# Keys, queries and cached values moved in more and smaller transfers

## The chip, the cores and the metric

The kernel runs on one core of a Trainium2 chip. The core has five engines that take their instructions in order, each from its own queue, and wait for one another on semaphores: TensorE (PE) multiplies matrices, VectorE (DVE), ScalarE (ACT) and GpSimd (POOL) do elementwise work, and SyncE (SP) only issues transfers between memory (DRAM) and the core's SBUF. The transfers themselves run on 16 DMA engines that all queues share. The metric is the device time of one launch in microseconds (us), the median of several runs; less is better.

## The reference

The reference is one inference step of a decoder trunk with two layers, for a prompt of 1024 tokens and eight samples of one token each that share the weights. Layer 0 is a convolution module beside a spatial gating unit; layer 1 is sparse attention with 16 query heads on 4 key and value (kv) heads of 64 numbers. Each layer is followed by an MLP. All is float32.

The part that matters here is layer 1. One projection gives queries, and keys and values for three branches, and three gates per head:

```python
z = h @ w_in
q, ck, cv, sk, sv, wk, wv, g = jnp.split(z, splits, axis=-1)
q_rot = rope(q, pos)
return q, q_rot, kvr(ck), kvr(cv), rope(kvr(sk), pos), kvr(sv), rope(kvr(wk), pos), kvr(wv), gates
```

Attention is a gated sum of three softmaxes: of the plain queries over compressed keys, of the rotated queries over the eight best blocks of 64 keys, and of the rotated queries over a window of 512 keys:

```python
o = g[..., 0:1] * o_cmp + g[..., 1:2] * o_sel + g[..., 2:3] * o_win
```

The samples do the same over paged caches and a window buffer of 512 rows, and the step returns that buffer moved on by one row (`kw[:, -nw:]`, `vw[:, -nw:]`).

## The kernel before

Features lie on the 128 partitions and tokens along the rows, so an activation is eight tiles of 128x1032 (1024 prompt tokens and 8 samples). A float32 product is made of three matmuls on numbers split in a high and a low part (`dense`, L278): for each weight tile 8 tiles of K x 3 chunks of tokens x 3 passes. Weights come through `granule` (L178): SP loads a raw tile (L180), ACT makes its high part (L175), POOL its low part (L176); nine slots, so three granules, are in the ring at once. All other SBUF tiles are slots of equal size, handed out the longest free first (`Slots`), so that the load of a tile waits for whoever last used its slot.

The order of the work on each engine is set when the kernel is built: a scheduler runs the program against a model of the chip and places each engine's instructions in one fixed order. SP issues its transfers in that order, and each of them waits, beside its data and its slot, on one of eight counters (DMAHW0 to DMAHW7) that SP's transfers use in turn.

Layer 1 goes in these steps:

- `project`: the tiles of the compressed branch, which are stored in DRAM (`cd`, L812); the keys of the selected and the window branch, two tiles each (the two halves of a head, four kv heads of 32 rows in a tile), rotated, split and written to DRAM as `kd` (L851); the queries, four groups of two tiles, of which the plain ones go to `qp` (L874) and the rotated ones, high and low part, to `qd` (L876). These writes are the spills. A tile holds (kv, r) on its partitions; in DRAM the kv head is outermost, so that later one kv head can be read by itself.
- Still in `project`: values and gates, nine tiles of tokens in three groups, each for two weights (`pvg`, L895 to L897), and in between `prompt_compress`, twice, which reads `cd` back as `pch` (L763) and its weights as `w1r` (L616) and multiplies them (`pc`, L641).
- `prompt_attention`: 32 units, of one kv head and 128 queries each, eight for a kv head. `load_k` (L950) loads the four key tiles of a kv head: window and selected, high and low part. Each has the 64 rows of the head twice, one copy below the other, since the queries carry their high parts over their low parts. The next head's keys are loaded at the end of the eighth unit. `load_q` loads a unit's queries (`pc<-qp` L962, `q<-qd` L964). The scores are `S<-K,q` (L1045), the values are multiplied one unit later (`tp` L1088, `op` L1102).
- `sample_attention`: its steps are spread over the units. `fetch_wv` loads the window's values (`wvr`, L1249), and POOL stores them moved on by one row to output 17 (L1252, L1253, L1255).

Of the kernel before, what the change touches and what calls it, by code (L numbers as in the profile page):

```python
# [15 lines left out]
P = 128  # L16
# [3 lines left out]
B = 8  # L20
# [11 lines left out]
class Slots:  # L32
    """Equal pieces of SBUF, handed out in the order of the trace, the longest free first."""
# [21 lines left out]
def body(tc, I, O, ctx):  # L55
# [48 lines left out]
    # One of a layer's six vectors at a time, over eight tiles of K: four groups of rows at once, for the halves  # L104
    # of its columns and for even and odd tiles.
# [30 lines left out]
    def ada_half(a):  # L136
        """Half of a vector's tiles."""
        l, j, h, ws, pl = a
        if h == 0:
            half_p[0] = mmps("pada")  # L140
        for n in (0, 2):
            ada_mm(half_p[0], 4 * h + n, ws[n:n + 2])
        pl.put(ws)
        if h == 1:
            ada_end(l, j, half_p[0])

    def ada_steps(vectors, pl):
        """Vectors (layer, number) two tiles at a time."""
        todo = [(l, j, k) for l, j in vectors for k in range(0, KT, 2)]

        def fetch(l, j, k):
            return [ada_raw(l, j, k + i, pl) for i in range(2)]

        ws = fetch(*todo[0])
        for n, (l, j, k) in enumerate(todo):
            if k == 0:
                p = auxps("pada")
            ada_mm(p, k, ws)
            pl.put(ws)
            if n < len(todo) - 1:  # L160
                ws = fetch(*todo[n + 1])
            else:
                ring.free.extend(pl.free)
            if k == KT - 2:
                ada_end(l, j, p)
            yield
# [19 lines left out]
    class Norm:  # L186
        """RMS norm of x, a chunk at a time; h = x * rstd * scale + shift as hi and lo parts, or the output."""
# [82 lines left out]
    def dense(pt, wh, wl, xh, xl, ks, woff, chunks, only=None):  # L270
        """pt[c] = W^T x over the tiles ks of K, the float32 product in three passes."""
        for n, k in enumerate(ks):
            if only not in (None, k):
                continue
            w0 = woff + k * 128
            for i, (w, v) in enumerate(((wh, xh), (wh, xl), (wl, xh))):
                for c in chunks:
                    pe.matmul(pt[c][:, :CH], w[:, w0:w0 + 128], v[k][:, c * CH:(c + 1) * CH],  # L278
                              start=n == 0 and i == 0, stop=n == len(ks) - 1 and i == 2)

    def lead(srcs, names):
        """Two tiles right after a norm: its last chunk comes last."""
        w = [granule(s) for s in srcs]
        pts = [[mmps(n) for _ in range(3)] for n in names]
        for pt, (wh, wl) in zip(pts, w):
            dense(pt, wh, wl, hh, hl, range(KT), 0, (0, 1))
        for k in range(KT):
            for pt, (wh, wl) in zip(pts, w):
                dense(pt, wh, wl, hh, hl, range(KT), 0, (2,), k)
        ring.put(*[t for p in w for t in p])  # L290
        return pts

    def resid(l, gi, mt, pt, c, first):
        """x += gate * y for one tile of features and one chunk."""
# [92 lines left out]
    def even(half):  # L387
# [62 lines left out]
        for i in range(4):  # L450
            # the samples: one position each
# [13 lines left out]
        for g in range(4):  # L465
            # keep s <= t (s on partitions)
            pool.affine_select(wsT[:, g, :], wsT[:, g, :], pattern=[[1, P]], compare_op=OP.is_ge, fill=0.0, base=0,
                               channel_multiplier=-1)
# [3 lines left out]
        # u  # L472
# [15 lines left out]
        def conv_norm(c):  # L488
            """Layer norm over the 512 channels of the convolution, silu."""
# [27 lines left out]
        # v, with the tokens on partitions  # L517
# [5 lines left out]
        def v_norm(tl):  # L523
            """Layer norm over the channels of a group's token tiles."""
# [78 lines left out]
    cmp_bias = {}  # L603

    def cmp_weights(kv, eng=None):
        """The compression's first weights as hi and lo parts, and the bias that its position term adds."""
# [26 lines left out]
    def compress_half(q, w, ch, jh):  # L633
        """The compression's hidden units [e, (k, c)], the part of half of the positions' pairs; ch: its (hi, lo)."""
# [16 lines left out]
    kcd = tc.dram_tile([P, 1024], FT, name="kcd")     # samples' compressed keys: (kv, r); b, half, c  # L651
    vcd = tc.dram_tile([P, 1024], FT, name="vcd")     # and values: (b % 2, c); b // 2, kv, d
# [3 lines left out]
    def gather(dst, src, i, q=None):  # L656
        """One page of a pool; src: the pool, its pages first."""
# [8 lines left out]
    class Units:  # L666
        """The compression of the samples' pages, one of keys and values and one sample at a time, in halves."""
# [16 lines left out]
        def prep(self, eng=None):  # L684
            """The next half of the positions' pairs as hi and lo parts."""
# [22 lines left out]
        def run(self):  # L708
            """Half a unit."""
# [34 lines left out]
    qd = tc.dram_tile([4, 2, 2, 32, 4, S], FR, name="qd").bitcast(FT)        # rotated: kv, hl, half, r, g, token  # L744
    qp = tc.dram_tile([4, 2, 2, 32, 2, S], FT, name="qp")                    # plain: kv, g // 2, half, r, g % 2, token
    kd = tc.dram_tile([2, 2, 4, 2, 32, S], FR, name="kd").bitcast(FT)        # sel/win, hl, kv, half, r, token
    cd = tc.dram_tile([2, 2, 2, 256, 512], FR, name="cd").bitcast(FT)        # k/v, hl, j2, (kv d), (jp c)
# [36 lines left out]
    def project(R):  # L784
# [3 lines left out]
        R["ks"] = cst.tile([P, 2, 2, B], FT, name="ks")         # half, sel/win, b  # L788
        R["cks"] = cst.tile([P, 4, B], FT, name="cks")
        R["qs"] = cst.tile([P, 2, 2, 4, B], FT, name="qs")      # rot/plain, half, g, b  # L790
# [8 lines left out]
        # the compressed branch's rows  # L799
# [18 lines left out]
        def rope(pa, pb, c, a1, a2, r1, r2, t):  # L818
            """The rotated halves of one chunk; a1, a2: copies of the plain ones."""
# [10 lines left out]
        for w in range(2):  # L830
# [18 lines left out]
            for half in range(2):  # L849
                for m in range(2):  # L850
                    sp.dma_start(kd[w, m, :, half], h[half][m][:, :S].bitcast(FT))  # L851
# [3 lines left out]
        # queries  # L855
        for g in range(4):
# [16 lines left out]
            for i in range(2):  # L873
                sp.dma_start(qp[:, g // 2, i, :, g % 2], qa[i][:, :S])  # L874
                for m in range(2):
                    sp.dma_start(qd[:, m, i, :, g], h[i][m][:, :S].bitcast(FT))  # L876
# [3 lines left out]
        # values and gates, with the tokens on partitions  # L880
# [34 lines left out]
    def topk_bias(out, score, nb, m8, mr):  # L915
        """out: 0 for the eight largest scores (ties: the lower index first), else -1e30."""
# [6 lines left out]
    def prompt_attention(R, psb):  # L923
# [21 lines left out]
        def load_k(kv):  # L945
            K = {}
            for w in (1, 0):
                for m in range(2):
                    t = sl.get("K", FR)
                    sp.dma_start(t[:, :S].bitcast(FT),  # L950
                                 kd[w, m, kv].rearrange("a r t -> (a r) t")[None].to_broadcast([2, 64, S]))
# [3 lines left out]
        def load_q(n):  # L955
            """The queries of the nth unit: rotated, hi over lo; plain, two heads over two."""
# [11 lines left out]
        class Unit:  # L968
            """The four heads of one kv head and 128 queries, the queries on partitions."""
# [57 lines left out]
            def score(self, w, g):  # L1027
                """One head's probabilities, in the window (w = 1) or the selected blocks."""
# [45 lines left out]
            def values(self):  # L1074
                """The steps of the product with the values."""
# [47 lines left out]
        def turned(i):  # L1123
            """The heads of the first kv heads again, as hi and lo parts."""
# [47 lines left out]
    def sample_attention(R, bank):  # L1172
        """All heads of the samples' one position: rows (b, h) on partitions. The steps, in their order: arithmetic
        and, in between, the fetches of what comes two steps later."""
# [68 lines left out]
        def fetch_wv(pp):  # L1243
            vr = held["wv", pp] = [sl.get("wvr") for _ in range(4)]
            for bp in range(4):
                v4 = vr[bp][:, :1024].rearrange("p (t b d) -> p t b d", t=2, b=2)
                for b2 in range(2):
# [3 lines left out]
                    if pp == 0:  # L1251
                        pool.dma_start(o17[0:127], v4[1:, 0, b2])  # L1252
# [11 lines left out]
        def compressed():  # L1264
            # the new token's keys
# [6 lines left out]
            # compressed keys  # L1272
# [65 lines left out]
        def turn():  # L1338
            """The probabilities with the keys on partitions."""
# [39 lines left out]
        def pick():  # L1379
            """Each head's own part of the values."""  # L1380
# [51 lines left out]
    # l: fetch a sample's pages, p, P: split half of them, r: compress half; x, y: fetch half of x;  # L1432
    # a: fetch half a vector's weights, A: its product; s: the norm's sums of a chunk, m: its output
# [65 lines left out]
def _layout(i):  # L1499
# [36 lines left out]
    q = wi[:, :1024].reshape(1024, 4, 4, 2, 32)          # kv, g, half, r  # L1536
    q = q.transpose(0, 2, 3, 1, 4).reshape(1024, 1024)   # (g, half) tiles of (kv, r)
# [6 lines left out]
    wo = f["odd_w_out"][0].reshape(4, 2, 2, 64, 1024)    # kv, hh, h2, d  # L1544
    r["odd_out"] = tiles(wo.transpose(0, 2, 1, 3, 4).reshape(1024, 1024))
    w1 = np.stack([f["cmp_w1_k"][0], f["cmp_w1_v"][0]])  # kv, (m, jp, j2), d, e
# [5 lines left out]
    pc = np.stack([f["cache_cmp_k"][0], f["cache_cmp_v"][0]]).reshape(2, 80, 8, 2, 4, 2, 4, 64)  # kv, page, c, jh, jp, j2, k, d  # L1552
    r["cache_cmp"] = c(pc.transpose(1, 5, 7, 0, 3, 6, 4, 2).reshape(80, 128, 512))
    sk = f["cache_sel_k"][0].reshape(80, 128, 4, 2, 32)   # page, pos, kv, half, r
# [72 lines left out]
```

## Time and profile before

| | |
|---|---|
| three runs | 3210.59, 3211.17 and 3217.25 us, median 3211.17 |
| profiled execution | span 3215.4 us from its first to its last instruction; the page has no other time for it |
| busy | PE 91%, DVE 50%, ACT 34%, POOL 32% of the span |
| mean granted TensorE clock | 0.951 |
| moved by DMA | 322.67 MB, 100 GB/s on the average |

The page gives the busy time of each engine, the span in 40 slices (a slice is 80 us here), the DMA queues, the chain of work that ended last, and the groups of instructions with what ended the idle time before them. The granted clock is TensorE's: 1.00 is its level of 2.4 GHz, 0.50 that of 1.2 GHz. The DMA share is the mean busy share of the 16 DMA engines. In a trace row `4x32x1024` or `128x128 f32` is the shape, `x4` the number of instructions merged, and `[49.18 <-ACT wh L175]` the idle time ahead and what ended it.

### The profile page before, as it was taken

What the parts mean: (1) busy time and instruction counts of PE and PEld (TensorE: products, weight loads), DVE (VectorE), ACT (ScalarE), POOL (GpSimd) and SP (SyncE); (2) the same over time, 40 slices, a digit from 0 to 9 for tenths busy, and PEclk for the clock granted to TensorE, in tenths of its full rate; (3) what the DMA queues carried; (4) which work ended last, traced back from release to release, by engine and by line L of the source; (5) the groups of instructions that cost most, each with busy time, mean ns of one, the idle gap of its engine ahead of it and who ended that gap; (6) DMA issues with size and microseconds to landing.
All of it is one profiled execution on the core that took longest, in us unless ns stands there. A gap on an engine that the chain in (4) does not pass through costs nothing.

```text
span 3215.4 us, 48262 instructions
## 1 busy us (share of the span) xinstructions
PE 2924.5 (91%) x18386; PEld 2565.8 (80%) x18386; DVE 1599.0 (50%) x3443; ACT 1099.0 (34%) x2366; POOL 1038.3 (32%) x747
## 2 busy tenths in 40 slices
PE   7887988999999999899268889699999999999997
PEld 5787778999999999899265444356679999999996
DVE  5799789322222223854106555367868322222227
ACT  4431265221112222532125545357754222211113
POOL 2655346222122122531333322143456222222224
PEclk9998999999999999999678988799999999999998
DMA  8323442322222221343453422251143111111113
GB/s 301 102 90 93 174 147 95 125 93 73 85 86 94 97 79 66 136 172 130 144 156 90 150 78 68 68 175 69 37 158 99 53 46 47 46 47 47 46 47 105
DMA packets 153384, 322.67 MB, mean 100 GB/s; under 512 B 20602, under 2 KB 85930, under 8 KB 153154
## 3 DMA queue, kind: packets, MB, share of 16 engines
q1 hardware_dynamic: 137266, 291.62, 27.0%
q0 software_dynamic: 7744, 23.42, 2.4%
q10 hardware_dynamic: 8144, 4.56, 0.6%
q8 instruction: 145, 2.38, 0.3%
q14 instruction: 85, 0.70, 0.1%
HBM read 271.46 MB, written 48.08 MB: 99 GB/s over the span
## 4 chain that ended last, share of the span: by engine, by line
PE 38%; DMA 8%; DVE 5%; SPq 1%; issue 1%; ACT 1%; POOL 0%; ACTq 0%; DVEq 0%; POOLq 0%
PE mm L278 22%; PE op L1102 4%; PE tp L1088 4%; PE S L1045 3%; DMA K<-kd 3%; DVE nacc L209 1%; PE sa L1375 1%; DMA qd<-qh 1%; DMA wr<-in_odd_vg_dram 1%; DMA q<-qd 1%; DMA qp<-qa 1%; PE sa L1209 1%; DVE nt L246 1%; DMA pch<-cd 1%; PE f L278 1%
## 5 line engine op out<-in xcount | busy, mean ns | idle before, releaser
L176 POOL TENSOR_TENSOR wl<-wr,wh 128x1024 fp32r<-128x1024 f32 (+2 forms) x250 | 630.8, 2526 | 1437.6 <-ACT wh L175 934.1
L175 ACT ACTIVATE wh<-wr 128x1024 fp32r<-128x1024 f32 (+2 forms) x250 | 259.7, 1039 | 1116.7 <-PE mm L278 609.5
L297 DVE SCALAR_TENSOR_TENSOR x<-mm,ada,x 128x344 f32<-128x344 f32 (+1 forms) x432 | 224.8, 566 | 439.3 <-PE mm L278 439.3
L278 PE MATMUL mm<-hh,wl 128*128 128x344 f32 x1824 | 432.3, 321 | 4.2 <-POOL wl L176 4.2
L278 PE MATMUL mm<-hh,wh 128*128 128x344 f32 x1824 | 432.9, 322 | 0.0
L278 PE MATMUL mm<-hl,wh 128*128 128x344 f32 x1824 | 430.1, 321 | 0.0
L278 PE MATMUL mm<-uh,wh 128*128 128x344 f32 x1536 | 348.7, 322 | 5.2 <-DVE x L297 5.2
L278 PE MATMUL mm<-uh,wl 128*128 128x344 f32 x1536 | 346.2, 321 | 2.2 <-POOL wl L176 2.2
L278 PE MATMUL mm<-ul,wh 128*128 128x344 f32 x1536 | 347.6, 321 | 0.0
L338 DVE SCALAR_TENSOR_TENSOR ffr<-mm,ffr 128x344 f32<-128x344 f32 x180 | 81.7, 510 | 525.5 <-ACT ffr L337 525.5
L278 PEld LDWEIGHTS mm<-hh,wh 128*128 128x128 f32 x1824 | 313.8, 188 | 18.8 <-DVE ffr L338 10.9
L278 PEld LDWEIGHTS mm<-hh,wl 128*128 128x128 f32 x1824 | 315.0, 188 | 5.6 <-POOL wl L176 5.0
L278 PEld LDWEIGHTS mm<-hl,wh 128*128 128x128 f32 x1824 | 315.1, 189 | 0.7 <-issue 0.5
L278 PEld LDWEIGHTS mm<-uh,wh 128*128 128x128 f32 x1536 | 262.6, 189 | 11.5 <-DVE ffr L338 5.0
L278 PEld LDWEIGHTS mm<-uh,wl 128*128 128x128 f32 x1536 | 262.1, 188 | 2.9 <-POOL wl L176 2.8
L278 PEld LDWEIGHTS mm<-ul,wh 128*128 128x128 f32 x1536 | 263.1, 189 | 0.7 <-issue 0.5
L1045 PE MATMUL S<-K,q 128*128 128x320 f32 (+5 forms) x768 | 186.3, 360 | 74.2 <-DMA K<-kd 71.6
L1063 POOL TENSOR_SCALAR p<-p,sm 128x640 f32<-128x640 f32 (+4 forms) x192 | 139.6, 743 | 281.8 <-DVE sm L1061 121.9
L1056 ACT ACTIVATE p<-p,sm 128x640 f32<-128x640 f32 (+7 forms) x256 | 186.2, 729 | 101.1 <-DVE sm L1055 96.4
L1045 PEld LDWEIGHTS S<-K,q 128*128 128x128 f32 x768 | 123.2, 197 | 102.6 <-DMA K<-kd 40.6
L1088 PEld LDWEIGHTS tp<-c_ident,p 128*128 128x128 f32 x1056 | 115.8, 144 | 104.6 <-issue 91.1
L406 DVE SCALAR_TENSOR_TENSOR C<-A,c_conv_w,C 128x1024 f32<-128x1024 f32 x120 | 191.8, 1638 | 1.6
(397 smaller groups left out, 4779.5 us busy)
## 6 DMA issues: line engine op xcount, KB each, us to landing
wr<-in_ffn_w_dram SPq DMA_DIRECT2D x144, 512.0 KB
adaw<-in_ada_w_dram SPq DMA_DIRECT2D x96, 512.0 KB
wr<-in_even_out_dram SPq DMA_DIRECT2D x24, 512.0 KB
wr<-in_odd_out_dram SPq DMA_DIRECT2D x24, 512.0 KB
graw<-in_cache_cmp_dram SPq DMA_DIRECT2D x92, 128.0 KB
x<-in_xT_dram SPq DMA_DIRECT2D x16, 512.0 KB
wr<-in_odd_in_dram SPq DMA_DIRECT2D x16, 512.0 KB
qd<-qh SPq DMA_DIRECT2D x16, 512.0 KB
```

Source lines behind the costliest of these rows:

```text
L175: act.activation(hi, raw, AF.Copy)
L176: (eng or dve).tensor_sub(lo, raw, hi)
L209: dve.tensor_add(a[:, :w], a[:, :w], s)
L278: pe.matmul(pt[c][:, :CH], w[:, w0:w0 + 128], v[k][:, c * CH:(c + 1) * CH], start=n == 0 and i == 0, stop=n == len(ks) - 1 and i == 2)
L297: dve.scalar_tensor_tensor(x[mt][:, c0:c1], pt[:, :w], g[:, 0:1], x[mt][:, c0:c1], op0=OP.mult, op1=OP.add)
L338: dve.scalar_tensor_tensor(r, pt[c][:, :CH], 0.0, r, op0=OP.max, op1=OP.mult)
L406: dve.scalar_tensor_tensor(o, A[:, j:j + S], conv_w[:, i, j:j + 1], o, op0=OP.mult, op1=OP.add)
L1045: pe.matmul(st[:, a0 + a, :hw], self.qr[g], self.K[w, m][:, k0 + a * hw:k0 + (a + 1) * hw], start=m == 0, stop=m == 1)
L1056: act.activation(p, p, AF.Exp, bias=nm[:, g:g + 1], scale=0.125, accum_out=sme[:, g:g + 1])
L1063: (pool if w or h < 2 else dve).tensor_scalar(self.p[w][h], self.p[w][h], rg[:, h:h + 1], 1.0, op0=OP.mult, op1=OP.mult)
L1088: pe.transpose(tp[:kk, g], src, ident)
L1102: pe.matmul(self.op[a * 64:a * 64 + 64, :256], v, ptv[:, a * 256:(a + 1) * 256], start=n == 0, stop=n == total - 1)
```

## The change

Three places issue more transfers for the same bytes. A spill of 128 partitions to a DRAM tensor whose outermost dimension is the kv head becomes four, one for each kv head of 32 rows. A key tile, before one transfer whose source has a dimension of two copies with a step of zero, becomes two of 64 rows. The store of the first 127 rows of the window's values becomes one of 112 rows and one of 15. Nothing else is edited but comments, which go; line numbers move by one to four behind L851.

```diff
             for half in range(2):
                 for m in range(2):
-                    sp.dma_start(kd[w, m, :, half], h[half][m][:, :S].bitcast(FT))
+                    for kv in range(4):
+                        sp.dma_start(kd[w, m, kv, half], h[half][m][kv * 32:kv * 32 + 32, :S].bitcast(FT))
...
             for i in range(2):
-                sp.dma_start(qp[:, g // 2, i, :, g % 2], qa[i][:, :S])
-                for m in range(2):
-                    sp.dma_start(qd[:, m, i, :, g], h[i][m][:, :S].bitcast(FT))
+                for kv in range(4):
+                    rows = slice(kv * 32, kv * 32 + 32)
+                    sp.dma_start(qp[kv, g // 2, i, :, g % 2], qa[i][rows, :S])
+                    for m in range(2):
+                        sp.dma_start(qd[kv, m, i, :, g], h[i][m][rows, :S].bitcast(FT))
...
                     t = sl.get("K", FR)
-                    sp.dma_start(t[:, :S].bitcast(FT),
-                                 kd[w, m, kv].rearrange("a r t -> (a r) t")[None].to_broadcast([2, 64, S]))
+                    for a in range(2):
+                        sp.dma_start(t[a * 64:a * 64 + 64, :S].bitcast(FT), kd[w, m, kv].rearrange("a r t -> (a r) t"))
...
                     if pp == 0:
-                        pool.dma_start(o17[0:127], v4[1:, 0, b2])
+                        pool.dma_start(o17[15:127], v4[16:, 0, b2])
+                        pool.dma_start(o17[0:15], v4[1:16, 0, b2])
                         pool.dma_start(o17[127:255], v4[:, 1, b2])
```

The order of SP in the query stage, where the last two groups of queries are spilled among the weights of the values (`odd_vg`) and of the compression (`w1r`), before:

```order
L876 DMA qd<-qh 4x32x1024 x4
L874 DMA qp<-qa 4x32x1024
L180 DMA wr<-in_odd_vg_dram 128x560
L874 DMA qp<-qa 4x32x1024
L180 DMA wr<-in_odd_vg_dram 128x840
L616 DMA w1r<-in_cmp_w_dram 128x1024
L876 DMA qd<-qh 4x32x1024 x4
L874 DMA qp<-qa 4x32x1024
```

and of the change:

```order
L879 DMA qd<-qh 32x1024 x16
L877 DMA qp<-qa 32x1024 x4
L180 DMA wr<-in_odd_vg_dram 128x560
L877 DMA qp<-qa 32x1024 x4
L180 DMA wr<-in_odd_vg_dram 128x840
L616 DMA w1r<-in_cmp_w_dram 128x1024
L879 DMA qd<-qh 32x1024 x16
L877 DMA qp<-qa 32x1024 x4
```

Each spill has become four at the same place; no load has moved past one here.

The order of SP at the first change of the kv head, with what each transfer waits for; `wkr` and `vcs` are loads of the samples' steps. Before:

```order
L950 DMA K<-kd 128x1x1024 [waits DMAHW2_49,PE_49,Pool_49]
L950 DMA K<-kd 128x1x1024 [waits DMAHW3_49,PE_49,Pool_49]
L1231 DMA wkr<-in_win_k_dram 128x2x512 [waits DMAHW4_49,PE_49,Activation_49]
L950 DMA K<-kd 128x1x1024 [waits DVE_49,DMAHW5_49,PE_49,Activation_49]
L950 DMA K<-kd 128x1x1024 [waits DMAHW6_49,PE_49,Activation_49]
L1261 DMA vcs<-vcd 64x2x256 [waits DMAHW7_49,DMASW6_49,PE_49]
```

and of the change:

```order
L954 DMA K<-kd 64x1024 [waits DMAHW6_49,PE_49,Pool_49]
L954 DMA K<-kd 64x1024 [waits DMAHW7_49]
L954 DMA K<-kd 64x1024 [waits DMAHW0_49,PE_49,Pool_49]
L1234 DMA wkr<-in_win_k_dram 128x2x512 [waits DMAHW1_49,PE_49,Activation_49]
L954 DMA K<-kd 64x1024 [waits DMAHW2_49]
L954 DMA K<-kd 64x1024 [waits DVE_49,DMAHW3_49,PE_49,Activation_49]
L954 DMA K<-kd 64x1024 [waits DMAHW4_49]
L1265 DMA vcs<-vcd 64x2x256 [waits DMAHW5_49,DMASW6_49,PE_49]
L1265 DMA vcs<-vcd 64x2x256 [waits DMAHW6_49]
L954 DMA K<-kd 64x1024 [waits DMAHW7_49,PE_49,Activation_49]
L954 DMA K<-kd 64x1024 [waits DMAHW0_49]
```

Each key tile is now two loads, of which the first waits for the slot; a load of `wkr` and two of `vcs` stand between the halves and the tiles.

## Rows read from the trace of the kernel before

**Rows 1.** The page: its head, TensorE's busy share and its granted clock in 40 slices, and the chain that ended last, by engine and by line.

```profile
span 3215.4 us, 48262 instructions
...
PE   7887988999999999899268889699999999999997
...
PEclk9998999999999999999678988799999999999998
...
PE 38%; DMA 8%; DVE 5%; SPq 1%; issue 1%; ACT 1%; POOL 0%; ACTq 0%; DVEq 0%; POOLq 0%
PE mm L278 22%; PE op L1102 4%; PE tp L1088 4%; PE S L1045 3%; DMA K<-kd 3%; DVE nacc L209 1%; PE sa L1375 1%; DMA qd<-qh 1%; DMA wr<-in_odd_vg_dram 1%; DMA q<-qd 1%; DMA qp<-qa 1%; PE sa L1209 1%; DVE nt L246 1%; DMA pch<-cd 1%; PE f L278 1%
```

**Rows 2.** Busy time of each engine (with instructions) in stretches of the span, then the granted clock, the DMA share and GB/s.

```profile
25.00:75.00 50.00, 46.18 (x349) 33.49 (x349) 28.59 (x63) 28.25 (x54) 10.75 (x20) 0.93 0.97 349
1425.00:1500.00 75.00, 75.00 (x480) 75.00 (x479) 40.42 (x83) 20.19 (x41) 14.67 (x11) 1.00 0.37 135
1512.00:1661.00 149.00, 77.70 (x538) 73.53 (x537) 17.22 (x45) 33.49 (x70) 50.21 (x33) 0.76 0.52 162
1525.00:1550.00 25.00, 0.00 (x0) 0.00 (x0) 0.72 (x3) 0.00 (x0) 0.00 (x0) 0.50 0.28 106
1625.00:1650.00 25.00, 23.55 (x182) 22.05 (x182) 1.67 (x10) 13.03 (x27) 17.05 (x16) 1.00 0.86 252
1661.00:1703.00 42.00, 10.73 (x108) 8.87 (x106) 6.53 (x48) 9.14 (x35) 4.29 (x10) 0.53 0.30 97
1703.00:1825.00 122.00, 120.10 (x737) 67.15 (x737) 89.25 (x330) 77.56 (x216) 42.87 (x55) 0.99 0.39 122
1825.00:1881.00 56.00, 28.54 (x134) 14.71 (x134) 12.46 (x59) 12.28 (x38) 8.26 (x14) 0.64 0.25 90
2024.00:2074.00 50.00, 23.08 (x116) 12.81 (x114) 9.81 (x47) 11.08 (x37) 6.72 (x11) 0.66 0.14 53
1350.00:1375.00 25.00, 25.00 (x161) 25.00 (x160) 11.50 (x11) 11.35 (x13) 12.31 (x9) 1.00 0.65 227
```

**Rows 3.** Pieces of the chain of waits in order of time: start, length, what.

```profile
1515.95 19.29 DMA qp<-qa
...
1554.78 12.18 DMA w1r<-in_cmp_w_dram
...
1827.12 24.54 DMA K<-kd
```

**Rows 4.** SP's queue in order of time in the query stage (start, length, transfers merged) and as the first unit begins, and the spread of two kinds of issue over the span or a stretch (least/median/most ns).

```profile
1458.83 15.51 SPq L876 DMA_DIRECT2D qd<-qh  x4
1474.43 4.72 SPq L874 DMA_DIRECT2D qp<-qa  x1
...
1491.18 15.07 SPq L876 DMA_DIRECT2D qd<-qh  x4
...
1645.53 1.91 SPq L664 DMA_DIRECT2D skr<-in_cache_sk_dram  x4
...
L876 SPq DMA_DIRECT2D qd<-qh x16: 516/2370/4732, 1458.8 to 1589.5; - x16
...
L180 SPq DMA_DIRECT2D wr<-in_odd_vg_dram x18: 327/336/6430, 1479.2 to 1643.6; - x18
```

**Rows 5.** TensorE at the first and the last of the 54 matmuls for values ahead of its standstill; the first of the three groups of these matmuls from 1512 to 1661, with its busy time, the mean ns of one, and the idle time ahead; and the matmuls of one compression in the chain.

```profile
1512.41 0.29 PE L895 MATMUL pvg<-wh,hh 128*128 128x280 f32 x1
...
1519.23 0.28 PE L897 MATMUL pvg<-wl,hh 128*128 128x280 f32 x1
...
L895 PE MATMUL pvg<-wh,hh 128*128 128x280 f32 x143 | 44.5, 312 | 50.1 <-ACT wh L175 50.0
...
1645.91 5.85 PE pc L641 x48
```

**Rows 6.** ScalarE's copies of the last group of queries, and VectorE's last splits of it.

```profile
1568.55 1.13 ACT L822 ACTIVATE qa<-pqb 128x344 f32<-128x344 f32 x3
...
1586.88 0.93 DVE L176 TENSOR_TENSOR qh<-qf,qh 128x344 fp32r<-128x344 f32 x2
```

**Rows 7.** TensorE at the first attention unit: the matmuls that it waited for.

```profile
1675.73 1.12 PE L990 MATMUL S<-kcx,pc 64*128 64x64 f32 x8 [14.02 <-DMA pc<-qp]
...
1687.12 0.45 PE L1045 MATMUL S<-K,q 128*128 128x128 f32 x1 [6.41 <-DMA K<-kd]
1698.37 2.28 PE L1045 MATMUL S<-K,q 128*128 128x128 f32 x7 [10.81 <-DMA K<-kd]
```

**Rows 8.** Who waited for whom from 1700 to 2200 (total us, times, longest), SP's own waits from 1800 to 2180, and TensorE at the first two key tiles of the first change.

```profile
PE S L1045 <- DMA K<-kd: 54.4, 8, 9.1
...
SPq L950 <- PE op L1102: 28.3, 3, 13.2
SPq L950 <- PE tp L1088: 28.2, 3, 11.0
...
1841.92 0.44 PE L1045 MATMUL S<-K,q 128*128 128x128 f32 x1 [9.11 <-DMA K<-kd]
...
1851.70 0.91 PE L1045 MATMUL S<-K,q 128*128 128x128 f32 x3 [7.24 <-DMA K<-kd]
```

**Rows 9.** The stores of the window's values: KB each and median us from issue to landing, and GpSimd's time for an issue (least/median/most ns).

```profile
out_dram<-wvr POOLq DMA_DIRECT2D x8, 128.0 KB, 4.5
out_dram<-wvr POOLq DMA_DIRECT2D x8, 127.0 KB, 4.3
...
L1252 POOL DMA_DIRECT2D out_dram<-wvr x8: 544/544/613, 2136.5 to 2147.7; - x8
```

## The prediction

> **What bounds the kernel now.** I read the page first, then the granted clock and DMA share by stretch, then the chain of waits in order of time, and last the DMA queue of SP. The page says that TensorE is busy for 91% of the span, at full clock nearly throughout, with a hole in the slices 18 to 22 and two smaller ones behind it [rows 1]. Outside these holes the kernel is bound by matmuls, and the change touches nothing there. The holes are the place to look: the chain that ended last runs through DMA for 8% of the span, some 257 us, and the keys `K<-kd` alone have 3% of it.
>
> By stretches [rows 2] the holes are four: the values and gates with the prompt's compression (1512 to 1661, 149 us, of which TensorE works 77.7), the first attention unit (1661 to 1703), and the first two changes of the kv head (1825 to 1881 and 2024 to 2074). Between them, from 1703 to 1825, TensorE is busy for 120.1 of 122 us. In the holes the reader should look at the two last columns. From 1525 to 1550 TensorE does nothing at all, and yet the DMA engines are busy for 0.28 of their time only, at 106 GB/s; 0.28 of 16 engines is 4.5. From 2024 to 2074 it is 0.14 and 53 GB/s, 2.2 of 16. From 25 to 75 the same engines reach 0.97 and 349 GB/s. So DMA is waited for while it runs at a third to a sixth of what it can. The shapes explain the two figures: the spills go out as 4x32x1024 and would fill four engines, the keys come in as two copies of 64 rows and would fill two. The chain in the holes is made of these transfers, or of loads that stand behind them on SP [rows 3].
>
> SP issues in order. A load of weights takes it 0.33 us at best, but in the query stage a spill of 512 KB takes 4.72 us [rows 4], and 512 KB in 4.72 us is 111 GB/s, the same rate again. A group of queries is six spills and two weight loads and took SP from 1458.83 to 1491.18, 32.4 us. TensorE needs for its two tiles 144 matmuls, at 480 in 75 us [rows 2] 22.5 us. So SP falls 10 us behind per group, unseen until TensorE runs out of weights at 1519 [rows 5].
>
> **The change part by part.** *Spills* (`kd`, `qp`, `qd`). 32 transfers become 128 of 32 rows and 128 KB; bytes and program places are the same. If 32 rows spread over all engines, the 16.8 MB no longer queue for four of them. Price on SP: no row shows a 32-row spill of 128 KB. The nearest is a 128 KB load, four in 1.91 us, 0.48 each [rows 4]; the ends are 0.33 (a weight load) and 2.37 (the median `qd` issue). I take 0.48: a group then has 24 spills and two weights, 26 x 0.48 = 12.5 us against TensorE's 22.5, which hides it. At 2.37 that cover is gone (a rival below).
>
> What is left of the hole from 1512 to 1661? TensorE's work in it is three groups of 143 matmuls for values and gates, 54 of which took from 1512.41 to 1519.23, 0.129 us each, so 55 us, and two times 48 compression rows at 5.85 us, in all 67 us [rows 5]. DMA's work is 149 us x 162 GB/s = 24.1 MB, at 349 GB/s 69 us. The two overlap. The loads of the compression stand on SP behind the spill of the last queries, and that behind their rotation: it took from 1568.55 to 1586.88 [rows 6], and I add these 18 us to the 69. 87 us instead of 149: 62 gained. Ends: 82 (TensorE alone bounds it), and 25 (24.1 MB at 227 GB/s, the rate from 1350 to 1375, plus 18 is 124 us).
>
> *First unit.* TensorE waits 14.0 us for the first queries and 6.4 and 10.8 us for keys, 31 us together [rows 7]. Twelve transfers from 1650 on are issued in 6 us, and with the four pages ahead 3.4 MB at 349 GB/s take 10, so the keys are there about as TensorE arrives (1661). I leave 7 us for the chain of the unit itself, which no row shows apart from the waits: 24 gained; ends 14 (only the first wait goes) and 36 (all but the matmuls, 10.7 us at a clock of 0.53, the lower level mostly).
>
> *Changes of the head.* The two stretches are 106 us long. TensorE waits 54.4 of them for keys, in eight waits [rows 8], and works 51.6 at a clock of 0.64 to 0.66, between its two levels of 1.2 and 2.4 GHz, which it drops to when it has sat idle. Their 250 matmuls at the pace of 1703 to 1825 (737 in 120.1) are 41 us, so 65 is the most to gain. The second tile now comes 10 us behind the first [rows 8]; at 349 GB/s all four take 6. But a key tile needs a free slot, and SP waits for TensorE before it issues half of them (28.3 and 28.2 us in all [rows 8]). These tiles are not sooner for a faster transfer. I leave 5 us of wait per change: 55 gained; lower end 27, where the third and fourth tile stay as late as now.
>
> The Trainium skill, DMA: Bandwidth & Descriptors, Rules for kernel authors, advises against just this, two transfers to the two halves of the partitions, since both use the same 16 engines and serialize. By that the changes of the head and the key waits of the first unit gain nothing (rival 2). The page's section on why a DMA increments its semaphore by 16 takes the premise away: the number of engines is the largest up to 16 that divides the slowest dimension of both sides, two here before and 16 after; the share of 0.14 agrees with the two, and no row of before shows the 16 for this load. I go by the row; 64-row loads run beside weights at 0.86 and 252 GB/s from 1625 to 1650 [rows 2].
>
> *Stores of cached values.* 127 rows become 112 and 15. Today these stores land in 4.3 us, the 128-row ones in 4.5 [rows 9]; there is nothing to gain. GpSimd issues eight more, 8 x 0.54 = 4.4 us, while it waits for the values' loads; I take 0, at worst 4.
>
> Also the scheduler places matmuls of the attention otherwise, since it reckons with other landings; the set of them is the same. The present order leaves TensorE idle for 2 of the 122 us from 1703 to 1825 [rows 2], so a better one has little to win; I take 0, and up to 10 us of loss over the attention as an estimate.
>
> **Sum.** 62 + 24 + 55 = 141 us off a span of 3215.4: 3074. The profiled execution's span lies 4 us above the median of the runs, 3211.17, so I forecast 3070.
>
> **The rivals.**
> 1. *The waits change hands.* Spills flow, but keys come late for want of slots: the lower ends of first unit and changes, 62 + 14 + 27 = 103, give 3108. For it: SP's waits for TensorE before keys. Against: part of these is TensorE's own standstill, which goes.
> 2. *Only the spills gain*: the two halves of a key tile queue for the same engines, and a tile still takes 10 us. 62 + 14 = 76, 3135. Against: the 0.14 of 2024 to 2074, which leaves most engines empty while keys are waited for.
> 3. *All of it goes*, and TensorE alone bounds the holes: 82 + 36 + 65 = 183, 3028. For it: between the holes TensorE is busy 98% [rows 2].
> 4. *No change*: the transfers are bound by memory, not by engines, and the pieces run as slowly: 3211. Against: 349 GB/s in the same trace.
> 5. *Slower: SP becomes the bound.* The transfers of SP share eight counters, and each waits for the one eight places ahead. If a 32-row spill holds SP as long as a whole one does now, 2.37 us, 128 take 303 us where the spills now take from 1407 to 1590, 183 us. That is 120 later, less 79 gained at keys: 41 slower, 3252. It decides from 2.05 us per spill ((183 + 79) / 128). Against: the 4.72 us are four engines' rate, and a 128 KB load shows 0.48 [rows 4]. The Trainium skill's page named above, Anatomy of one DMA, has a fixed 2.0 us per transfer and would have small ones coalesced; 112 more of them one after another would be 224 us, an estimate from that page, but transfers here overlap.
>
> **How the numbers follow.** Forecast 0.58 (3045 to 3095 by itself), rival 1 0.16, rival 2 0.04, rival 3 0.15, rival 4 0.03, rival 5 0.04. All lower ends together give 66, 3145, all upper ones 3028; 3030 to 3130 leaves out rivals 2, 4 and 5 and the edges of 1 and 3, about 0.18. A measurement here tells 0.2% (6 us) from no change. Faster: 0.58 + 0.16 + 0.04 + 0.15 = 0.93; same 0.03; slower 0.04.
>
> **What would show it.** Right: the DMA share from the key spill to the first unit is well above 0.5 wherever TensorE waits; SP's 32-row issues are near 0.5 us; the standstill of 50 us before the values [rows 5] is gone; TensorE's key waits fall from 54.4 us [rows 8] to under 15; the span to the first `kd` spill and from the last kv head on is the same. Wrong: spills at 2 us or more each on SP; key waits as long as now, with SP waiting for TensorE; or the holes closed but new waits on VectorE and ScalarE in the units of the same length.

## The result, and the profile after

The change runs in 3064.24 us (median of 4 runs, 3056.66 to 3069.77) against 3211.89 us for the kernel before: ratio 0.954, 95% interval 0.9522 to 0.9558. The forecast was 3070, the range 3030 to 3130. In a later comparison on one chip it took 3063.57 us, ratio 0.9545 (0.953 to 0.956).

The page of the changed kernel, as in [rows 1]: its head, TensorE's busy share and granted clock by slices of 77 us, and the chain that ended last by engine.

```profile
span 3061.6 us, 48413 instructions
...
PE   7898789999999999989989999999999999999997
...
PEclk9999899999999999999999998999999999999998
...
PE 71%; DVE 12%; DMA 2%; ACT 2%; issue 1%; SPq 0%; POOL 0%; ACTq 0%; DVEq 0%; POOLq 0%
```

The hole of the slices 18 to 22 is gone, DMA has fallen from 8% of the chain to 2%, and the mean granted clock is 0.976 instead of 0.951. Busy time by stretch, as in [rows 2] (PE, PEld, DVE, ACT, POOL, then granted clock, DMA share, GB/s): the query stage; the values and gates, and once more by itself the stretch 1525 to 1550 in which TensorE stood still before; the first unit; the units behind it; and the first two changes of the kv head.

```profile
1425.00:1500.00 75.00, 75.00 (x480) 75.00 (x479) 50.76 (x102) 25.20 (x51) 17.21 (x11) 1.00 0.67 191
1509.00:1602.00 93.00, 75.37 (x540) 72.27 (x539) 27.41 (x41) 33.32 (x69) 48.82 (x32) 0.89 0.78 209
1525.00:1550.00 25.00, 18.15 (x116) 17.95 (x115) 11.91 (x8) 6.20 (x16) 12.68 (x9) 0.78 0.74 190
1602.00:1626.00 24.00, 20.84 (x180) 14.49 (x179) 19.07 (x97) 16.65 (x57) 8.08 (x14) 0.86 0.40 119
1626.00:1739.00 113.00, 111.04 (x686) 61.34 (x684) 78.87 (x294) 74.10 (x202) 42.04 (x54) 1.00 0.42 130
1739.00:1758.00 19.00, 17.84 (x123) 9.65 (x123) 12.01 (x49) 10.91 (x35) 5.70 (x10) 1.00 0.92 245
1901.00:1919.00 18.00, 16.41 (x100) 8.69 (x98) 8.84 (x43) 10.00 (x37) 3.83 (x7) 0.91 0.48 123
```

The stage of values has about as many matmuls as before (540 and 538) in 93 us instead of 149. A change of the head took some 50 us with DMA at 0.25 and 0.14 [rows 2]; now it takes 18 to 19 us at 0.92 and 0.48.

To compare kernels whose spans are shifted, I cut TensorE's rows in order of time at the same work: the first matmul for the keys (`pka`), the first and last matmul for values (`pvg`), the first score on compressed keys of certain units, and the first matmul of the output projection. Units are counted from 1, so the second kv head begins with unit 9 and the third with unit 17. Lengths in us; the last two columns are experiments told below.

| From, to | before | change | spills only | key loads only |
|---|---|---|---|---|
| `pka` to first `pvg` | 135.6 | 135.6 | 135.6 | 135.6 |
| first to last `pvg` (values stage) | 149.0 | 92.9 | 93.4 | 148.9 |
| last `pvg` to unit 3 (first unit and what leads to it) | 57.5 | 24.3 | 56.4 | 27.8 |
| unit 3 to 9 | 113.3 | 112.7 | 112.7 | 116.2 |
| unit 9 to 10 (first change of the head) | 50.6 | 19.4 | 53.4 | 18.1 |
| unit 10 to 17 | 145.1 | 142.3 | 144.3 | 142.3 |
| unit 17 to 18 (second change) | 48.7 | 18.4 | 49.7 | 18.6 |
| unit 18 to the output projection | 285.8 | 289.0 | 283.3 | 283.8 |

The spans differ by 153.8 us: 56.1 in the values stage, 33.2 at the first unit, 31.2 and 30.3 at the changes, and 3.0 elsewhere in net. These 3.0 are no gain of the change: 3.2 us of difference lie ahead of `pka` (1376.8 and 1373.6), where nothing was changed, and the three other rows of units and the end come to -0.2 in net. So much is scatter between two profiled executions.

SP's queue in the query stage, as in [rows 4] (start, length, transfers merged), and the spread of one kind of spill over the span.

```profile
1449.56 8.21 SPq L879 DMA_DIRECT2D qd<-qh  x16
1457.87 1.92 SPq L877 DMA_DIRECT2D qp<-qa  x4
1459.88 0.38 SPq L180 DMA_DIRECT2D wr<-in_odd_vg_dram  x1
1465.88 1.70 SPq L877 DMA_DIRECT2D qp<-qa  x4
...
L879 SPq DMA_DIRECT2D qd<-qh x64: 302/420/1052, 1449.6 to 1539.4; - x64
```

Four times as many spills hold SP for 8.21 us where four whole ones held it for 15.51 [rows 4]. A group of queries is 8.21 + 1.92 + 1.70 and two weights at 0.38, 12.6 us of SP instead of 32.4.

### The profile page after: what moved, and what is told of

Read it like the earlier page. It is cut to its first block, busy times and chain, and to the rows that moved or that the text cites. A ratio compares the mean times of both kernels' runs of the same rounds, so it can differ in the third digit from the quotient of the medians.

```text
span 3061.6 us, 48413 instructions
## 1 busy us (share of the span) xinstructions
PE 2901.6 (95%) x18386; PEld 2554.6 (83%) x18386; DVE 1619.2 (53%) x3443; ACT 1100.7 (36%) x2366; POOL 1047.0 (34%) x755
## 4 chain that ended last, share of the span: by engine, by line
PE 71%; DVE 12%; DMA 2%; ACT 2%; issue 1%; SPq 0%; POOL 0%; ACTq 0%; DVEq 0%; POOLq 0%
PE mm L278 45%; PE op L1105 5%; PE tp L1091 5%; PE S L1048 4%; DVE nacc L209 2%; PE pqa L278 1%; DVE nt L246 1%; PE pqb L278 1%; PE f L278 1%; PE pada L115 1%; DVE hl L252 1%; PE pck L278 1%; DVE x L297 1%; DVE C L406 1%; PE sa L1379 1%
## 5 line engine op out<-in xcount | busy, mean ns | idle before, releaser
L278 PEld LDWEIGHTS mm<-hh,wh 128*128 128x128 f32 x1824 | 314.6, 189 | 18.7 <-DVE ffr L338 10.9
L1091 PE MATMUL tp<-c_ident,p 128*128 128x128 f32 x1056 | 174.8, 287 | 2.5 <-POOL p L1066 1.7
```

The lines of the kernel that those rows point to most:

```text
L1091: pe.transpose(tp[:kk, g], src, ident)
```

## The experiments

Each kernel ran beside the kernel before on the same chip; ratios are to that.

**Spills alone** (against before):

```diff
-                    sp.dma_start(kd[w, m, :, half], h[half][m][:, :S].bitcast(FT))
+                    for kv in range(4):
+                        sp.dma_start(kd[w, m, kv, half], h[half][m][kv * 32:kv * 32 + 32, :S].bitcast(FT))
```

and the same for `qp` and `qd`; keys and stores as before.

> Only the spills kd, qp and qd are cut into four by kv head; keys and stores as before. Theory (what counts is over how many DMA engines one transfer is spread, and the parts add up): the stage of values and gates falls from 149 to about 93 us and the first queries no longer wait, the key waits of the two changes of the head stay near 54 us; 3211 - 56 - 16 = 3139, 3125 to 3150. Rival (the finer pieces help by the other order that the scheduler makes, over the whole attention): under 3100, or a key wait that falls too.

Measured: 3155.57 us, 0.9828 (0.9811 to 0.9845), 55.5 us less than before and 5.6 above the expected range. The values stage shrank as in the change, 93.4 us, but the first unit hardly gained (56.4 against 57.5). TensorE's matmuls there that waited, and SP's queue just ahead of them:

```profile
1615.49 1.12 PE L993 MATMUL S<-kcx,pc 64*128 64x64 f32 x8 [12.61 <-DMA pc<-qp]
1627.87 0.44 PE L1048 MATMUL S<-K,q 128*128 128x128 f32 x1 [7.40 <-DMA K<-kd]
1639.17 2.34 PE L1048 MATMUL S<-K,q 128*128 128x128 f32 x7 [10.86 <-DMA K<-kd]
```

```profile
1590.28 1.52 SPq L953 DMA_DIRECT2D K<-kd  x2
1591.92 7.92 SPq L965 DMA_DIRECT2D pc<-qp  x1
1599.90 2.41 SPq L967 DMA_DIRECT2D q<-qd  x1
1602.37 6.58 SPq L965 DMA_DIRECT2D pc<-qp  x1
1609.06 5.91 SPq L953 DMA_DIRECT2D K<-kd  x2
```

These are the three waits of [rows 7], still 12.6, 7.4 and 10.9 us. The first is a wait for queries, yet cutting the queries' spills hardly shortened it (14.0 before): behind two key tiles the small loads of queries hold SP for 7.9, 2.4 and 6.6 us.

**Key loads alone** (against before):

```diff
-                    sp.dma_start(t[:, :S].bitcast(FT),
-                                 kd[w, m, kv].rearrange("a r t -> (a r) t")[None].to_broadcast([2, 64, S]))
+                    for a in range(2):
+                        sp.dma_start(t[a * 64:a * 64 + 64, :S].bitcast(FT), kd[w, m, kv].rearrange("a r t -> (a r) t"))
```

> Only the key loads are cut into two of 64 rows; spills and stores as before. Theory: the two changes of the head give their 61 us and the first unit the 17 us of its two key waits, the stage of values and gates stays at 149 us; 3211 - 78 = 3133, 3125 to 3155. Rival (two halves of a key tile queue for the same engines): 3200 to 3211, key waits as before.

Measured: 3116.46 us, 0.9703 (0.9682 to 0.9723), 94.6 us less than before and 8.5 below the expected range, since the first unit gave 29.7 us and not 17. SP's queue as the first unit begins, and TensorE's one wait for DMA there of 0.5 us or more:

```profile
1646.30 2.40 SPq L951 DMA_DIRECT2D K<-kd  x4
1648.80 0.57 SPq L962 DMA_DIRECT2D pc<-qp  x1
1649.48 2.46 SPq L951 DMA_DIRECT2D K<-kd  x4
1651.98 0.60 SPq L964 DMA_DIRECT2D q<-qd  x1
```

```profile
PE S L1045 <- DMA q<-qd: 2.9, 1, 2.9
```

The same query loads are now issued in 0.6 us, with uncut spills. So the wait for queries of [rows 7] came from the key tiles ahead of them. Rival 2, by which two halves of a key tile gain nothing, is refuted: the changes of the head fell to 18.1 and 18.6 us.

**As many transfers, cut along the tokens** (against before): the counts and bytes of the change, but each piece keeps the full partition pattern.

```diff
+                    for kv in range(4):
+                        ts = slice(kv * 256, kv * 256 + 256)
+                        sp.dma_start(kd[w, m, :, half, :, ts], h[half][m][:, ts].bitcast(FT))
...
+                    for a in range(2):
+                        ts = slice(a * 512, a * 512 + 512)
+                        sp.dma_start(t[:, ts].bitcast(FT),
+                                     kd[w, m, kv, :, :, ts].rearrange("a r t -> (a r) t")[None].to_broadcast([2, 64, 512]))
```

and the same for `qp` and `qd`; the stores as in the change.

> As many transfers as the change and as many bytes in each, but cut along the tokens: a spill into four of 4x32x256, a key tile into two of 2x64x512, each with the outermost dimension of before. Theory of the engines: nothing is gained, the DMA share in the holes is again 0.28 and 0.14, key waits 54 us or more; 3200 to 3260. Rival (more and smaller pieces, or the scheduler's other order, do it): near 3064.

Measured: 3221.63 us (7 runs), 1.0038 (1.0026 to 1.0049), 0.4% slower than before. Busy time in its query stage and in its second change of the head:

```profile
1425.00:1500.00 75.00, 72.59 (x463) 72.31 (x462) 36.80 (x76) 19.98 (x40) 14.58 (x10) 1.00 0.38 129
...
2027.00:2073.00 46.00, 20.06 (x108) 10.59 (x106) 8.55 (x44) 10.33 (x37) 3.60 (x7) 0.67 0.17 62
```

The DMA shares, 0.38 and 0.17, are those of the kernel before (0.37 and 0.14 [rows 2]), not those of the change. More transfers, smaller pieces and another order bring nothing as long as the outermost dimension stays. TensorE's key waits were 37.2 us from 1600 to 2100, less than the 54 expected, with 33.6 us of wait for queries beside them. The rows of these pieces are also shorter, 1 and 2 KB instead of 4, which this run alone does not tell from the outermost dimension; the next run keeps rows of 4 KB.

**Pieces of 64 rows** (against the change): a spill in two pieces, each with two kv heads outermost.

```diff
-                    for kv in range(4):
-                        sp.dma_start(kd[w, m, kv, half], h[half][m][kv * 32:kv * 32 + 32, :S].bitcast(FT))
+                    for kv in range(0, 4, 2):
+                        sp.dma_start(kd[w, m, kv:kv + 2, half], h[half][m][kv * 32:kv * 32 + 64, :S].bitcast(FT))
```

and the same for `qp` and `qd`.

> Spills cut into two of 64 rows with two kv heads outermost instead of four of 32; keys and stores as the change. Theory of the engines: two engines for a spill instead of four before and sixteen in the change, so the spills run at 53 GB/s; 16.8 MB take some 317 us, until about 1720 instead of 1593, and the first unit starts some 130 us later than before; less the 61 us of the head changes and 17 us of the first unit, 3211 + 130 - 78 = 3263, 3220 to 3320: slower than before in spite of smaller pieces. Rival (a finer cut helps by degrees): between 3064 and 3133.

Measured: 3282.79 us, 1.0224 (1.0206 to 1.0242), slower than before by 72 us although keys and stores are those of the change. Busy time in its query stage (which lasts longer here, so the stretch is a later one), SP's queue there, and TensorE's longest wait up to the end of the values:

```profile
1470.00:1590.00 120.00, 50.53 (x286) 49.02 (x285) 25.52 (x56) 12.98 (x26) 9.01 (x5) 0.73 0.18 67
```

```profile
1441.65 35.62 SPq L852 DMA_DIRECT2D kd<-kh  x8
...
1503.76 19.73 SPq L879 DMA_DIRECT2D qd<-qh  x5
```

```profile
PE pvg L898 <- ACT wh L175: 114.5, 4, 99.3
```

The rows of ScalarE name the weight's high part; what was late is the weight, behind spills of 4 us each. With two heads outermost the share is 0.18 and 67 GB/s (0.21 and 78 from 1425 to 1500), with four it was 0.37 and 135 [rows 2], with 32 plain rows it is 0.67 and 191. The number of pieces does not order the three.

How many DMA engines a piece reaches can be counted in the traces as the DMA packets that are in flight at one moment, if an engine has one at a time. From 1441.65 to 1477, a stretch of spills in each kernel, there were exactly two for 79% of the time in this kernel and exactly four for 73% before; in the change 16 are the commonest number. From 2030 to 2070, where key tiles were loaded before, there were exactly two for 82% of the time. With the pieces cut along the tokens the commonest numbers are four and two again. The counts that DMA adds to a transfer's semaphore agree: 16 for every 32-row spill and half key tile of the change, 5 for every spill before and 3 for every key tile before and every spill here, which fits four and two engines and one count more. So the number of engines is counted here and not only worked out from the DMA share, and the stage is the faster the more of them a piece reaches.

**Stores alone**: 127 rows as 112 and 15, the rest as before.

> Only the stores of the window's values are cut, 127 rows into 112 and 15. Theory: they landed in 4.3 us before, as the whole ones do, and nothing waits for them; no change, 3205 to 3217. Rival (127 rows run on few engines, or eight more issues on GpSimd hold up the attention): 4 us or more to either side.

Measured: 3218.21 us (10 runs) against 3213.51 (13 runs), 1.0013 (1.0002 to 1.0025): no gain, and a loss of some 4 us, with 0.6 to 8 us in the interval. The three parts alone come to 55.5 + 94.6 - 4.7 = 145 us, the change took 148.

**One transfer per spill by another layout** (against the change): with the kv head inside, `kd` as `[2, 2, 2, 4, 32, S]` and `qd` and `qp` alike, a spill is one transfer of 128 plain rows; loads of keys and queries become pieces of 32 rows.

```diff
-                    for kv in range(4):
-                        sp.dma_start(kd[w, m, kv, half], h[half][m][kv * 32:kv * 32 + 32, :S].bitcast(FT))
+                    sp.dma_start(kd[w, m, half].rearrange("k r t -> (k r) t"), h[half][m][:, :S].bitcast(FT))
...
-                    for a in range(2):
-                        sp.dma_start(t[a * 64:a * 64 + 64, :S].bitcast(FT), kd[w, m, kv].rearrange("a r t -> (a r) t"))
+                    for a in range(4):
+                        sp.dma_start(t[a * 32:a * 32 + 32, :S].bitcast(FT), kd[w, m, a % 2, kv])
```

> The buffers qd, qp and kd with the kv head inside the halves, so that a spill is one transfer of 128 rows again, 32 instead of 128, and keys and queries are loaded in pieces of 32 rows (64 instead of 32 for keys, 256 instead of 64 for queries). Theory (it is the engines per transfer, not the number of transfers): as fast as the change, 3064, 3050 to 3075. Rival (many small spills are what helps, or 192 more loads in the attention hold SP up): 3090 or more.

Measured: 3065.85 us, 0.9527 (0.9497 to 0.9558), the change's time. A spill as one transfer is as good as a spill in four, when its rows lie outermost. The stages are not those of the change: the values stage is shorter (83.6 us), the first unit (30.2) and the first change (23.5) are longer; the loads in smaller pieces are part of this run, and it does not tell what they cost.

**What is left of the hole.** In the change the values stage takes 92.9 us for 67 of matmuls. TensorE is busy for 75.2 of them, part of it at the lower of its two clock levels, 1.2 GHz (0.89 granted in the mean), and waits 17.5. These waits, ScalarE's copies with which the rotation of the last queries begins, VectorE's splits with which it ends, and GpSimd's rows at that time:

```profile
PE pc L641 <- DMA pch<-cd: 6.8, 1, 6.8
PE pc L641 <- ACT gates L914: 6.4, 1, 6.4
PE pvg L900 <- POOL wl L176: 4.3, 1, 4.3
```

```profile
1512.05 1.13 ACT L822 ACTIVATE qa<-pqb 128x344 f32<-128x344 f32 x3
```

```profile
1527.02 9.71 DVE L176 TENSOR_TENSOR qh<-qf,qh 128x344 fp32r<-128x344 f32 x2
```

```profile
1518.74 8.34 POOL L176 TENSOR_TENSOR wl<-wr,wh 128x840 fp32r<-128x840 f32 x2 [3.05 <-PE pvg L900]
...
1528.14 1.39 POOL L176 TENSOR_TENSOR wl<-wr,wh 128x560 fp32r<-128x560 f32 x1
...
1530.04 2.42 POOL L176 TENSOR_TENSOR w1l<-w1r,w1h 128x1024 fp32r<-128x1024 f32 x1
1532.40 3.95 POOL L176 TENSOR_TENSOR wl<-wr,wh 128x840 fp32r<-128x840 f32 x2
```

Two splits that took 0.93 us before [rows 6] take 9.71, and end at 1536.7, 0.4 us behind GpSimd's row of splits. The last spill of queries waits for them, and `pch` and weights stand behind it on SP. Two remedies, each alone and then both, against the change: the low parts of `odd_vg` on VectorE, and the loads of `pch` issued by ScalarE.

```diff
-                    wh, wl = granule(I["odd_vg"][n, :, k0 * 280:(k0 + kn) * 280], width=kn * 280)
+                    wh, wl = granule(I["odd_vg"][n, :, k0 * 280:(k0 + kn) * 280], width=kn * 280, eng=dve)
```

```diff
-                    sp.dma_start(t[j2 * 64:j2 * 64 + 64, :1024].rearrange("p (k x) -> p k x", k=4).bitcast(FT),
+                    act.dma_start(t[j2 * 64:j2 * 64 + 64, :1024].rearrange("p (k x) -> p k x", k=4).bitcast(FT),
```

> The change, with the low parts of the values' weights made by VectorE instead of GpSimd. In the profile of the change two splits of the last queries took VectorE 9.7 us instead of 0.9, while GpSimd made such low parts. Theory (the two engines hold each other up, and the spill and the loads behind it wait for it): the splits take 1 us again, the spill is issued 9 us earlier, 3064 - 9 = 3055, 3045 to 3060. Rival (the load moves to VectorE, which then is late): 3060 or more.

Measured: 3059.64 us, 0.9525 (0.95 to 0.9549). The spread of these splits on VectorE over the span, in the change and in this kernel (ns, least/median/most):

```profile
L176 DVE TENSOR_TENSOR qh<-qf,qh x24: 492/501/9284, 1448.9 to 1527.4; 128x344 fp32r<-128x344 f32 x16, 128x336 fp32r<-128x336 f32 x8
```

```profile
L176 DVE TENSOR_TENSOR qh<-qf,qh x24: 493/505/515, 1448.5 to 1526.0; 128x344 fp32r<-128x344 f32 x16, 128x336 fp32r<-128x336 f32 x8
```

The 9.28 us split is gone and the values stage falls to 79.3 us, 13.6 less. The units behind give most of it back: 3.5 us at the first unit and 5.9 from unit 3 to 9; why they do was not taken apart.

> The change, with the compression's loads pch issued by ScalarE instead of SyncE. Theory (what is left of the hole of values and gates, 93 us against 67 of matmuls, is loads behind the last queries' spill in SP's order): they come before that spill ends, the wait of 6.9 us for pch and part of the 12.7 and 8.5 us waits for values' weights go, 3064 - 10 = 3054, 3045 to 3060. Rival (that stage is bound by the bytes or by ScalarE and GpSimd): 3060 or more.

Measured: 3060.31 us, 0.9519 (0.9494 to 0.9543), values stage 88.3 us. The stage gained 4.6, the whole nothing that can be told from the change; 10 were expected.

> The change itself once more, to stand on one chip beside the next two kernels. 3057 to 3070 us, about 0.954 of before; values and gates stage (first to last matmul of the values) 93 us.

> The change, and both remedies for what is left of its hole at the values at once: the low parts of odd_vg on VectorE and the loads of pch issued by ScalarE. If the two waits stand one behind the other, the values stage falls below the 79 us that the first remedy alone left, to about 75 (matmuls alone are 67), and the kernel to about 3054; if TensorE's other limits give it back in the attention, as they did for the first remedy alone, the time is that of the change, 3057 to 3066.

> The layout of kd, qd and qp by which a spill is one transfer of 128 rows and the loads are 32-row pieces, and the low parts of odd_vg on VectorE. The layout alone had a values stage of 84 us and the change's time; if what the stages gain is given back in the attention, 3055 to 3066; if not, 3045 to 3052.

Measured on one chip, 5 runs each: the change 3063.57 us, 0.9545 (0.953 to 0.956); both remedies 3053.02 (3049.74 to 3057.69), 0.9508 (0.9493 to 0.9522); the other layout with the splits on VectorE 3060.25, 0.9532 (0.9519 to 0.9546). Both remedies together beat the change by 10.5 us, 0.3%, with intervals that do not meet. The mechanism that I expected of them is not what the rows show: the values stage took 83.6 us, not 75, with 7.3 us of waits for `pch`. Cut as in the table, its profiled execution and that of the change in this comparison differ by 6.5 us: 9.1 gained at the values, 4.1 at the first change of the head, 7.7 given back in the other units, and 1.1 ahead of `pka`, where nothing was changed. So the forecast of 3054 was met in part by luck. In the other layout with the splits on VectorE the values stage is 73.8 us, nearest to the 67 of all, and the kernel gains 3 us, with intervals that overlap: of 18.8 us gained at the values 6.2 are given back at the first unit, 5.4 at the first change and 3.5 between the changes. What a stage gains is not what the kernel gains.

## Why the prediction was right

**What bounded the holes** was named rightly: transfers that reach few engines, not memory, not SP and not the number of transfers. Only the outermost dimension of a piece, and with it the number of engines, orders the runs: 67 GB/s with two rows of heads outermost, 129 to 135 with four, 191 with 32 rows. Rival 4 (no change) falls with it, and rival 5 (SP the bound) with the median issue of 0.42 us, where the point of decision was 2.05. The fixed 2.0 us per transfer that rival 5 took from the Trainium skill (DMA: Bandwidth & Descriptors, Anatomy of one DMA) is given there for transfers issued by GpSimd, and it is no time of SP's here: a 32-row spill lands 2.5 us after its issue (median), and the next is issued after 0.42. The 0.48 us taken from the nearest 128 KB load was a good neighbour: 12.5 us of SP per group of queries were worked out, 12.6 measured.

The Trainium skill gave two rules on this. DMA: Bandwidth & Descriptors, Why a DMA increments its semaphore by 16 and not by 1, has the number of engines by what divides the slowest dimension; with 2, 4 and 32 outermost these runs agree (two, four and mostly 16 packets in flight). The advice against two transfers to two halves (Rules for kernel authors on the same page) did not hold here, where the one transfer that it prefers had two copies outermost: the key loads alone gained 94.6 us.

**The terms of the sum.** *Values stage*: 62 predicted, 56.1 measured; 93 us are left, not 87. The term added 69 us of transfers at full rate and 18 of rotation, and that it came so near is in part luck. The transfers were not what filled the stage: 19.4 MB went in it at 209 GB/s, not 24.1 at 349, and TensorE's 75.2 us of work and 17.5 of waits did. The rotation took 24.7 us to the end of its last split (1512.05 to 1536.73), 19.3 before; 5.2 of those 19.3 were VectorE's wait for a spill, and the new time has a hold-up of VectorE by GpSimd that the term lacked. The run with the splits on VectorE shows that to be worth more than the missing 6 us (79.3).

*First unit*: 24 predicted, 33.2 measured, near the upper end of 36. The step that failed is the split of its waits into 14 us for queries, gained by the spills, and 17 for keys. Spills alone gained 1.1 us here and key loads alone 29.7. The wait bore the name of the query tile, but the load was held on SP behind key tiles (6.6 and 7.9 us for an issue, 0.6 behind key tiles cut in two). So the lower end "only the first wait goes" was no real case, and my 76 us for rival 2 had 14 too many: of the 62 left, spills alone gained 55.5.

*Changes of the head*: 55 predicted, 61.5 measured, near the most to gain (65). I had left 5 us per change for key tiles that wait for a slot, and half of rival 1 rests on such waits. TensorE's waits for keys from 1600 to 2100, and SP's own waits at the key loads from 1680 to 2100:

```profile
PE S L1048 <- DMA K<-kd: 1.8, 4, 0.7
```

```profile
SPq L954 <- PE tp L1091: 25.7, 4, 13.7
...
SPq L954 <- PE op L1105: 8.1, 4, 4.5
```

SP still waits for TensorE there, about 34 us against 56.5 [rows 8], and TensorE no longer waits for keys: 1.8 us against 54.4. So SP's wait for a slot was no sign of a late tile, once the tile itself lands quickly (4.8 us in the median of the half tiles).

*Stores* 0, at worst 4, and some 4 us of loss measured (0.6 to 8); *reorder* 0, and 0.1 us in net over the units outside the holes. The sum of 141 against 153.8 of span is 12.8 low: 5.9 too much at the values, 9.2 and 6.5 too little at the first unit and the changes, and 3 of scatter. Rival 3 (all of it goes, 183) did not come about: 26 us still lie between the values stage and its 67 us of matmuls.

**One sign was stated too broadly.** The DMA share was to be well above 0.5 wherever TensorE waits. It is 0.74 in the standstill of old, but 0.40 at the first unit, where 20.84 of 24 us are work; the longest wait among the scores there, 2.5 us, is for VectorE.

## What to carry to other kernels

Where an engine waits for DMA while the DMA share is low (0.14 to 0.37 here), look at the outermost dimension of the transfer on both sides: 2 or 4 there confined it to as many engines here, and cutting it so that plain rows lie outermost, or laying out the DRAM tensor so, removed 148 us either way at unchanged bytes. Cutting the same bytes along another dimension gained nothing, and cutting into pieces that still have 2 outermost made it slower. A wait that bears one tile's name can belong to a transfer ahead of it on the same queue; SP's issue times show which.

## What the runs showed that I had not expected

VectorE and GpSimd hold each other up. GpSimd's two splits of 128x840 took 8.34 us while VectorE was working, and 3.95 while VectorE's split stood; that split took 9.28 instead of 0.5, and a copy of 128x8 took 1.95 instead of 0.16. The 8.34 and a copy of 1.93 are in the kernel before as well, where VectorE's splits of queries were never over 0.51. The Trainium skill, SBUF — State Buffer, Who interferes with whom, says that a VectorE instruction with two inputs in SBUF contends with a GpSimd instruction that reads SBUF; the runs agree. The page's summary has the later one blocked until the first finishes; here VectorE stood until GpSimd's whole row of four splits was through, so the price was many times one instruction. That moving the splits off GpSimd takes it away is shown; that a port is the cause is the page's word, and no run here tells it from another.
